# Key products of a pair of heads in two PSUM banks, issued alternately from the two row halves of the array

## The chip, the cores and the metric

The program runs on one core of one Trainium2 chip. The metric is the device time of one execution in microseconds (us). Three executions of the kernel before took 2318.74, 2316.63 and 2325.38 us (median 2318.74).

## What is computed

Two blocks, one after the other, on 512 latent and 256 context positions of width 1024. The first block has an RWKV-7 layer and a differential attention layer; the second has two hybrid attention layers. The change lies in the RWKV-7 layer, in which every one of 16 heads of 64 carries a 64x64 state along the positions, once forward and once backward:

```python
def step(S, inp):
    r_t, w_t, k_t, v_t, kk_t, a_t = inp
    sa = jnp.einsum("bhvk,bhk->bhv", S, kk_t)
    S = (S * w_t[:, :, None, :]
         - sa[..., None] * (kk_t * a_t)[:, :, None, :]
         + v_t[..., None] * k_t[:, :, None, :])
    return S, jnp.einsum("bhvk,bhk->bhv", S, r_t)
```

The streams r, k, v and the decays come from one projection of the normalised input (`h @ w_in`, 34 blocks of 128 columns) with a token shift and two low-rank products; the read-out normalises, gates and projects the result.

## The kernel before

The recurrence is done in chunks of 64 positions. `scan` weaves several generators into one program; each `yield` hands over to the next by a table of virtual times. A scheduler then fixes the order of the instructions on each engine, so what stands in the queues is neither the text's order nor decided on the chip. The parts that matter here:

- **Projection** (`Scan.dense`, `Scan.project`, matmul at L246). Each of the 34 projections has two groups of 24 matmuls of 384 columns, one PSUM bank per group (`pj`, tag "pj", `PJ` = 4 banks). ScalarE takes a bank out (L296 and L297; L351 and L352 for the gate, the last projection of each of eight feature blocks). `px` (tag "x", `6 - PJ` = 2 banks) serves the transposes of the values (L341, copied at L343) and the norms. After the eight blocks come the memory keys and values (`memory`, transposes at L400).
- **Preparation** (`Scan.prep` and `Scan.products`), 48 times: four pairs of feature blocks, three groups of four chunks, two blocks, two directions. The low-rank products go to a bank `ps_g` (L526). Then `products` multiplies the pair's keys: for head h = 0, which lies in partitions 0 to 63, four matmuls (L579), one per chunk, with 64 rows of contraction, 128 stationary and 128 moving columns, into the one bank `ps_b`; VectorE masks that bank out in three instructions (L585 to L587); then the same for h = 1 from partitions 64 to 127. Four transposes (L584) go to `ps_g` and ScalarE copies them (L590). A float32 matmul stands as two records in the trace, so a preparation has 16 records of L579.
- **Inversion** (`Scan.invert`), six times, one for eight preparations: an elimination of 31 steps on VectorE and GpSimd (from the transpose L641 over L655 and L657 to the transpose L661) and then four rounds of small matmuls (L669, L669, L682, L682) through the bank `ps_v` (`psv`) with copies between.
- **Chain** (`Scan.chain`), 48 steps, each one chunk for eight states (c0 at L733, c1 at L768, further products at L744, L757, L778, L791). Steps 4k to 4k+3 need inversion k // 2. Preparation n from the 25th on is put after step 4 (n // 4 - 3) in the program, so the two take turns.
- **Read-outs** and pieces of the modulation (`ada`, L85) run beside the chain; after it comes the dense part (L1079 and on), which has no line of the change.

PSUM has eight banks. During the projection: `ps_g` and `ps_b` in the pool `ppa`, four `pj` and two `x`. During the chain: `ppa` keeps its two, and `ppb` has six: the chain's three, `ps_m`, a second `ps_g` and `ps_v`. `psg` takes `ppa` and `ppb` in turn, and as each preparation asks twice, its low-rank products always get the one and its transposes always the other.

Of the kernel before, what the change touches and what calls it, by code (L numbers as in the profile page):

```python
# [8 lines left out]
FT = mybir.dt.float32  # L9
# [6 lines left out]
PSUM = bass.MemoryType.PSUM  # L16
# [189 lines left out]
class Scan:  # L206
# [14 lines left out]
        return self.pp.tile([128, 512], FT, name="ps_pj", tag="pj", bufs=PJ)  # L221

    def px(self):
        return self.pp.tile([128, 512], FT, name="ps_x", tag="x", bufs=6 - PJ)

    def s3(self, name):
        return self.dp.tile([128, 768], FT, name=name, tag="s3", bufs=SB)
# [254 lines left out]
        return pool.tile([128, 512], FT, name="ps_g", tag="g", bufs=1)  # L482

    def psv(self):
        if CH == 2 and self.ppb:
            return self.psm()
        return (self.ppb or self.ppa).tile([128, 512], FT, name="ps_v", tag="v" if self.ppb else "g", bufs=1)

    def psm(self):
        return self.ppb.tile([128, 512], FT, name="ps_m", tag="m", bufs=1)  # L490
# [72 lines left out]
    def products(self, p, g, jd, n, up, bk, al):  # L563
        E, nc = self.E, self.E.nc
        V, A, P = nc.vector, nc.scalar, nc.tensor
        b, u0 = n // 8, n % 8 * 4
# [5 lines left out]
        mask = self.maskg[:, 0:64].unsqueeze(1).to_broadcast([128, 4, 64])  # L572
        mask_r = self.maskg[:, 64:128].unsqueeze(1).to_broadcast([128, 4, 64])
        rbk = up.tile([128, 2, 4, 64], FT, name="rbk", bufs=8)
        for h, q in ((0, 0), (1, 64)):
            pb = self.ppa.tile([128, 4, 128], FT, name="ps_b", tag="b", bufs=1)
            e, o = q + 64, 64 - q
            for c in range(4):
                P.matmul(pb[:, c, :], bk[q:e, c].rearrange("p s t -> p (s t)"), al[q:e, c, h:3:2 - h, :], start=True,  # L579
                         stop=True, tile_position=(q, 0))  # L580
            if h:
                ps = self.psg()
                for c in range(4):
                    P.transpose(ps[:, c * 128:c * 128 + 128], bk[:, c].rearrange("p s t -> p (s t)"), E.ident)  # L584
            V.tensor_tensor(lb[q:e, u0:u0 + 4, :], pb[q:e, :, 0:64], mask[q:e], OP.mult)  # L585
            V.tensor_tensor(al[o:o + 64, :, h, :], pb[o:o + 64, :, 0:64], mask[o:o + 64], OP.mult)
            V.tensor_tensor(rbk[:, h], pb[:, :, 64:128], mask_r, OP.mult)  # L587
            yield 0
# [341 lines left out]
TB, TV = 3, 3  # L930
XB, OB = 2, 5
AN, AB, AT, AP = 0, 1, 7, -300
PJ = 4
BG = 1
VSB = 1
ZO = 0
# [3 lines left out]
CH = 1  # L940
# [3 lines left out]
def scan(E, stack):  # L944

    tc = E.tc
    right = dict(side="right", bufs=1, reuse_waits="tile")
    left = dict(bufs=1, reuse_waits="tile")
    S = Scan(E)
    ada = [(0, m) for m in range(16, 24)] + [(1, m) for m in range(24)]  # L950
    with ExitStack() as k, ExitStack() as t, ExitStack() as a:
# [24 lines left out]
        def early():  # L976
# [2 lines left out]
            pool = stack.enter_context(tc.tile_pool(name="dn", **left))  # L979
            D.append(Dense(E, pool, stack.enter_context(tc.tile_pool(name="dn_ps", space=PSUM, **left))))  # L980
            S.pt = t.enter_context(tc.tile_pool(name="tp", **left))
            D[0].W.split(0)
            yield lambda: S.read >= 3
            D[0].load_y(E.Y, 0, 6, 2)
# [945 lines left out]
```

## Time and profile before

| | us |
|---|---|
| median of three executions | 2318.74 |
| the profiled execution's own time | 2326.66 |
| its span, first to last instruction | 2324.6 |
| TensorE busy (PE) | 2106.3 (91%) |
| VectorE busy (DVE) | 1567.2 (67%) |
| ScalarE busy (ACT) | 1167.2 (50%) |
| GpSimd busy (POOL) | 686.0 (30%) |
| matmuls of L579, 768 records | 127.4 |
| mean granted TensorE clock | 0.93 |

Busy time counts a stretch once if several records overlap in it. The trace's durations of matmuls include the way through the array, so two matmuls in a row overlap in it and the distance between their starts is what a matmul costs the engine. The granted clock is 1.00 at 2.4 GHz and 0.50 at 1.2 GHz.

### The profile page before, as it was taken

To read this page: it belongs to the slowest core of one execution; us is meant where nothing else is said; L and a number is where in the kernel's file an instruction comes from. 1 tells how busy PE (TensorE), PEld (TensorE's weight loads), DVE (VectorE), ACT (ScalarE), POOL (GpSimd) and SP (SyncE) were. 2 spreads that over 40 slices of the span, in tenths; PEclk is the share of its full clock that TensorE was granted. 3 is DMA by queue.
4 is the path that set the end of the run, shared out by engine and by line. 5 is a ranking of instruction groups with operands and counts; after the bars stand their busy time and mean duration, and the time that the engine had idled before them with its cause. 6 is when DMAs were issued, how large, how long until landed. Compare 5 with 4: busy or idle time off the path is not lost.

```text
span 2324.6 us, 49071 instructions
## 1 busy us (share of the span) xinstructions
PE 2106.3 (91%) x18920; PEld 1867.2 (80%) x18920; DVE 1567.2 (67%) x3937; ACT 1167.2 (50%) x2634; POOL 686.0 (30%) x993
## 2 busy tenths in 40 slices
PE   7999999986899988886989999997899998999989
PEld 3989899975776776664888898987788987888878
DVE  5478868986288877723487767864676674677673
ACT  4455456563255544331255565664455564466652
POOL 0133523433036262321222223323223232032321
PEclk9999999986998788887999999998999999999999
DMA  7467456347544333153321111121312222321132
GB/s 245 136 204 227 144 188 216 105 151 230 184 135 130 90 110 101 54 181 93 134 93 55 47 58 44 42 85 48 114 64 82 67 78 91 119 80 66 60 100 82
DMA packets 190713, 263.60 MB, mean 113 GB/s; under 512 B 16145, under 2 KB 137489, under 8 KB 190353
## 3 DMA queue, kind: packets, MB, share of 16 engines
q1 hardware_dynamic: 190480, 260.48, 34.9%
q8 instruction: 149, 2.44, 0.4%
q14 instruction: 84, 0.68, 0.1%
HBM read 197.24 MB, written 63.18 MB: 112 GB/s over the span
## 4 chain that ended last, share of the span: by engine, by line
PE 47%; DVE 13%; DMA 4%; ACT 3%; issue 3%; POOL 1%; SPq 1%; ACTq 0%; DVEq 0%; POOLq 0%
PE ps_pj L1079 26%; PE ps_s L1376 3%; PE ps_m L85 2%; PE ps_t L1759 2%; PE ps_b L579 1%; PE ps_t L1586 1%; PE ps_s L1079 1%; PE ps_t L1745 1%; DMA w_raw<-in_wd_dram 1%; PE ps_t L1346 1%; DMA w_raw<-att 1%; PE ps_t L1575 1%; DVE ut L657 1%; PE ps_o L744 1%; PE ps_c L733 1%
## 5 line engine op out<-in xcount | busy, mean ns | idle before, releaser
L1079 PE MATMUL ps_pj<-w_hi,act 128*128 128x256 f32 x3264 | 645.5, 292 | 17.9 <-ACT act L1459 4.6
L1079 PEld LDWEIGHTS ps_pj<-w_hi,act 128*128 128x128 f32 x3264 | 529.5, 195 | 31.0 <-ACT act L1459 6.7
L1079 PE MATMUL ps_pj<-w_lo,act 128*128 128x256 f32 x1632 | 470.8, 289 | 0.0
L1079 PEld LDWEIGHTS ps_pj<-w_lo,act 128*128 128x128 f32 x1632 | 319.1, 196 | 0.6 <-issue 0.2
L246 PE MATMUL ps_pj<-h,b_hi 128*128 128x384 f32 (+1 forms) x1216 | 316.6, 341 | 2.7 <-ACT gh L352 1.5
L246 PEld LDWEIGHTS ps_pj<-h,b_hi 128*128 128x128 f32 x1216 | 220.0, 193 | 8.6 <-ACT gh L352 2.7
L246 PE MATMUL ps_pj<-h,b_lo 128*128 128x384 f32 (+1 forms) x608 | 206.9, 341 | 0.3 <-DVE b_lo L190 0.3
L1058 ACT CAST w_hi<-w_raw 128x1024 fp32r<-128x1024 f32 x120 | 121.0, 1050 | 58.9 <-DMA w_raw<-in_wd_dram 28.4
L1060 DVE TENSOR_TENSOR w_lo<-w_raw,w_hi 128x1024 fp32r<-128x1024 f32 x90 | 122.7, 1371 | 41.0 <-ACT w_hi L1058 40.3
L1079 PE MATMUL ps_pj<-act,w_hi 128*128 128x256 f32 x768 | 146.2, 286 | 0.0
L1735 POOL TENSOR_SCALAR p<-p,r 128x128 f32<-128x128 f32 (+2 forms) x64 | 71.8, 1122 | 239.3 <-DVE r L1729 156.7
L1060 POOL TENSOR_TENSOR w_lo<-w_raw,w_hi 128x1024 fp32r<-128x1024 f32 x30 | 72.8, 2428 | 234.3 <-ACT w_hi L1058 234.3
L579 PE MATMUL ps_b<-al,bk 64*128 64x128 f32 x768 | 127.4, 309 | 12.2 <-DVE rbk L587 10.7
L579 PEld LDWEIGHTS ps_b<-al,bk 64*128 64x128 f32 x768 | 105.7, 208 | 33.9 <-issue 21.0
L1079 PEld LDWEIGHTS ps_pj<-act,w_hi 128*128 128x128 f32 x768 | 120.9, 191 | 0.4 <-issue 0.2
L246 PEld LDWEIGHTS ps_pj<-h,b_lo 128*128 128x128 f32 x608 | 117.1, 193 | 3.6 <-issue 1.3
L547 POOL TENSOR_TENSOR s<-bk,src 64x256 f32<-64x256 f32 x96 | 76.9, 801 | 126.8 <-DVE bk L544 114.3
L1079 PE MATMUL ps_pj<-act,w_lo 128*128 128x256 f32 x384 | 109.6, 286 | 0.0
L1302 POOL TENSOR_TENSOR hx<-hx,ctab 128x256 f32<-128x256 f32 x80 | 68.0, 870 | 139.7 <-DVE ht L1300 82.5
L1565 POOL TENSOR_TENSOR p<-p 128x768 f32<-128x768 f32 x32 | 61.1, 1908 | 155.2 <-ACT p L1564 95.2
L1376 PE MATMUL ps_s<-k_s,q_hi 128*128 128x256 f32 (+2 forms) x256 | 91.2, 365 | 15.3 <-ACT p L1555 5.7
L85 PE MATMUL ps_m<-ada_s,cs 128*2 128x128 f32 x512 | 76.7, 314 | 13.4 <-DMA ada_s<-in_ada_w_dram 11.8
(323 smaller groups left out, 4920.0 us busy)
## 6 DMA issues: line engine op xcount, KB each, us to landing
w_raw<-in_wd_dram SPq DMA_DIRECT2D x120, 512.0 KB, 4.4
b_raw<-in_blocks_dram SPq DMA_DIRECT2D x84, 256.0 KB, 3.0
src<-streams SPq DMA_DIRECT2D x48, 384.0 KB, 3.6
ada_s<-in_ada_w_dram SPq DMA_DIRECT2D x32, 512.0 KB, 4.4
vs<-streams SPq DMA_DIRECT2D x48, 256.0 KB, 3.4
ada_w<-in_ada_w_dram SPq DMA_DIRECT2D x8, 1024.0 KB, 11.2
lr<-lora SPq DMA_DIRECT2D x96, 64.0 KB, 3.0
streams<-k SPq DMA_DIRECT2D x32, 192.0 KB, 2.8
```

The lines of the kernel that those rows point to most:

```text
L85: nc.tensor.matmul(ps[0:2, 0:128 * n], E.cs[:, kb, :], w(kb), start=(kb == 0), stop=(kb == 7))
L246: E.nc.tensor.matmul(ps[gi][:, :m], w[:, kb % 4, :], h[:, kb, :], start=(n[gi] == 1), stop=(n[gi] == 24))
L547: G.tensor_tensor(v3(rev(s))[a:a + 64], ut[a:a + 64, 1 if a == 0 else 0], v3(rev(r))[a:a + 64], OP.mult)
L579: P.matmul(pb[:, c, :], bk[q:e, c].rearrange("p s t -> p (s t)"), al[q:e, c, h:3:2 - h, :], start=True, stop=True, tile_position=(q, 0))
L1058: nc.scalar.copy(hi[:, a:a + 4], raw)
L1060: e.tensor_tensor(lo[:, a:a + 4], raw, hi[:, a:a + 4], OP.subtract)
L1079: E.nc.tensor.matmul(ps, a(kb), b(kb), start=(k == 0), stop=(k == 23))
L1302: G.tensor_tensor(w4(x), w4(x), cb, OP.mult)
L1376: P.matmul(ps, q[i][:, 2 * j + h, c], k[h][:, j, a:a + n], start=(i == 0), stop=(stop and i == 1))
L1565: G.tensor_tensor(ps_[0], ps_[0], ps_[1], OP.add)
L1735: G.tensor_scalar(t, t, r[:, h:h + 1], None, OP.mult)
L1759: P.matmul(ps[h * 64:h * 64 + 64, :128], v[:, kb, o:o + 64], pt[:, h, kb, :], start=(kb == 0), stop=(kb == nk - 1), tile_position=(0, h * 64))
```

## The change

The h = 0 and h = 1 products go to two banks (tags "b0" and "b1"), are written in one loop over the chunks, and so alternate between rows 0 to 63 and rows 64 to 127 of the array; VectorE's masking follows behind all eight. The bank for it is taken from two places. `PJ` falls from 4 to 3 and `px` keeps two banks. During the chain, `ps_v` has no bank of its own and shares `ppb`'s `ps_g` (tag "g"); at the end, when `ppa` is closed, a pool of its own (`tp_ps`) gives `psv` a bank.

```diff
     def px(self):
-        return self.pp.tile([128, 512], FT, name="ps_x", tag="x", bufs=6 - PJ)
+        return self.pp.tile([128, 512], FT, name="ps_x", tag="x", bufs=5 - PJ)
...
     def psv(self):
-        if CH == 2 and self.ppb:
-            return self.psm()
-        return (self.ppb or self.ppa).tile([128, 512], FT, name="ps_v", tag="v" if self.ppb else "g", bufs=1)
+        if self.pt:
+            return self.ppt.tile([128, 512], FT, name="ps_v", tag="v", bufs=1)
+        return (self.ppb or self.ppa).tile([128, 512], FT, name="ps_v", tag="g", bufs=1)
...
         rbk = up.tile([128, 2, 4, 64], FT, name="rbk", bufs=8)
+        pbs = [self.ppa.tile([128, 4, 128], FT, name="ps_b", tag="b%d" % h, bufs=1) for h in range(2)]
+        for c in range(4):
+            for h, q in ((0, 0), (1, 64)):
+                P.matmul(pbs[h][:, c, :], bk[q:q + 64, c].rearrange("p s t -> p (s t)"), al[q:q + 64, c, h:3:2 - h, :],
+                         start=True, stop=True, tile_position=(q, 0))
         for h, q in ((0, 0), (1, 64)):
-            pb = self.ppa.tile([128, 4, 128], FT, name="ps_b", tag="b", bufs=1)
-            e, o = q + 64, 64 - q
-            for c in range(4):
-                P.matmul(pb[:, c, :], bk[q:e, c].rearrange("p s t -> p (s t)"), al[q:e, c, h:3:2 - h, :], start=True,
-                         stop=True, tile_position=(q, 0))
+            pb, e, o = pbs[h], q + 64, 64 - q
...
-PJ = 4
+PJ = 3
...
             S.pt = t.enter_context(tc.tile_pool(name="tp", **left))
+            S.ppt = t.enter_context(tc.tile_pool(name="tp_ps", space=PSUM, **left))
```

Lines behind L578 move on by one (L579 becomes L578, L584 L585, L669 L670, L682 L683, L733 L734, L768 L769). The scheduler's order changes in the whole program.

TensorE's queue during the projection, at the end of the second gate and the start of the next projection, whose two groups are `ps_pj_1477` and `ps_pj_1478`. Before, the second group began while the first was still running, and here stand rows of the first group's end with the first head's burst of one preparation:

```order
L246 MATMUL ps_pj_1477<-h_97,b_lo_1436 128x384
L246 MATMUL ps_pj_1477<-h_97,b_hi_1435 128x384
L579 MATMUL ps_b_1771<-al_1723,bk_1647 128x128 x3
L341 MATMUL ps_x_1367<-ident_75,vr_1363 128x128 x4
L579 MATMUL ps_b_1771<-al_1723,bk_1647 128x128
L584 MATMUL ps_g_1797<-ident_75,bk_1647 128x128 x4
L246 MATMUL ps_pj_1477<-h_96,b_hi_1435 128x384
```

Now, the last four products of the same preparation (the four ahead of them read the same), and the same transposes L341:

```order
L578 MATMUL ps_b_1771<-al_1723,bk_1647 128x128
L578 MATMUL ps_b_1772<-al_1723,bk_1647 128x128
L578 MATMUL ps_b_1771<-al_1723,bk_1647 128x128
L578 MATMUL ps_b_1772<-al_1723,bk_1647 128x128
L585 MATMUL ps_g_1797<-ident_75,bk_1647 128x128 x4
L341 MATMUL ps_x_1367<-ident_75,vr_1363 128x128 x4
L526 MATMUL ps_g_1850<-lr_1851,lw_1445 128x256
L526 MATMUL ps_g_1850<-lr_1854,lw_1445 128x256
L246 MATMUL ps_pj_1478<-h_97,b_hi_1403 128x384
```

The first group is complete before the burst, the eight products of both heads stand together and alternate between the two banks, and the second group starts only behind the transposes L341.

TensorE's queue in the chain at the fourth inversion (`ps_v`), step 24 of the chain. Before:

```order
L584 MATMUL ps_g<-ident,bk 128x128 x4
L669 MATMUL ps_v<-ut,lb 32x32 x32
L579 MATMUL ps_b<-al,bk 128x128 x4
L866 MATMUL ps_m<-bdc,sq 128x2 x4
L526 MATMUL ps_g<-lr,lw 128x256 x2
L682 MATMUL ps_v<-lb,ut 32x32 x32
L860 MATMUL ps_m<-osum,bd_102 128x512
L579 MATMUL ps_b<-al,bk 128x128 x4
L584 MATMUL ps_g<-ident,bk 128x128 x4
```

Now:

```order
L683 MATMUL ps_v<-lb,ut 32x32 x32
L85 MATMUL ps_m<-ada_s,cs 2x128 x8
L769 MATMUL ps_c<-rhs,lb 64x64
L683 MATMUL ps_v<-lb,ut 32x32 x32
L90 MATMUL ps_m<-ident,ada_r 128x2
L769 MATMUL ps_c<-rhs,lb 64x64 x7
L779 MATMUL ps_z<-xz,bkt 64x64
L792 MATMUL ps_o<-rbk,xz 64x64
L85 MATMUL ps_m<-ada_s,cs 2x128 x8
L779 MATMUL ps_z<-xz,bkt 64x64 x7
L792 MATMUL ps_o<-rbk,xz 64x64 x7
L585 MATMUL ps_g<-ident,bk 128x128 x4
```

Before, preparations stand between the inversion's rounds, and 37 were through their products ahead of the first round; now none stands between them, 34 are through, and the transposes of the 33rd (`ps_g`) come behind the last round. At the fifth inversion 45 were through before and 42 are now; at the sixth all 48 in both, but the sixth comes at step 38 of the chain before and at step 40 now, the 48th preparation at step 34 and now at step 38. When the last matmul of L246 is issued, 20.5 preparations stood ahead of it before and 24 now.

## Rows read from the trace of the kernel before

**Rows 1.** Busy time by stretch: start:end and length, engines, granted clock, DMA share, GB/s.
```profile
121.00:506.00 385.00, 377.52 (x2728) 347.85 (x2727) 312.12 (x655) 216.59 (x450) 148.16 (x271) 0.97 0.56 180
506.00:545.00 39.00, 23.34 (x98) 17.72 (x98) 29.15 (x70) 17.57 (x33) 12.46 (x27) 0.57 0.62 199
...
642.00:770.00 128.00, 117.81 (x1520) 92.89 (x1517) 107.05 (x249) 65.02 (x152) 63.36 (x130) 0.91 0.44 132
770.00:816.00 46.00, 43.78 (x469) 33.52 (x464) 36.94 (x87) 24.04 (x45) 7.46 (x12) 0.67 0.24 69
...
924.00:986.00 62.00, 52.45 (x978) 42.12 (x973) 43.26 (x116) 25.52 (x43) 20.73 (x66) 0.89 0.20 57
...
1108.00:2324.60 1216.60, 1119.72 (x8762) 1043.68 (x8761) 813.08 (x2216) 655.49 (x1565) 324.83 (x269) 0.96 0.23 77
```

**Rows 2.** The same view, PE and PEld alone, of L246, then of L579.
```profile
121.00:506.00 385.00, 278.88 (x1488) 252.81 (x1488) 0.97 0.56 180
121.00:506.00 385.00, 48.31 (x328) 40.21 (x328) 0.97 0.56 180
```

**Rows 3.** Timeline of PE, a burst of L579 alone: start, length, engine, line.
```profile
145.65 0.60 PE L246 MATMUL ps_pj<-h,b_hi 128*128 128x384 f32 x2
146.18 1.16 PE L579 MATMUL ps_b<-al,bk 64*128 64x128 f32 x8
147.26 0.45 PE L246 MATMUL ps_pj<-h,b_lo 128*128 128x384 f32 x1
```

**Rows 4.** Timeline of PE, L526 and L579 from opposite row halves.
```profile
707.73 0.48 PE L526 MATMUL ps_g<-lr,lw 64*128 64x256 f32 x1
707.74 0.48 PE L579 MATMUL ps_b<-al,bk 64*128 64x128 f32 x2
...
708.51 0.38 PE L579 MATMUL ps_b<-al,bk 64*128 64x128 f32 x2
```

**Rows 5.** Timeline of ACT at the second gate's first bank.
```profile
167.28 0.59 ACT L343 COPY vt<-ps_x 128x512 f32<-128x512 f32 x1 [1.70 <-PE ps_x L341]
...
168.14 0.50 ACT L352 ACTIVATE gh<-ps_pj 128x384 f32<-128x384 f32 x1
```

**Rows 6.** By stretch, L246 alone: a gate's last matmul to its first bank's release.
```profile
160.40:168.70 8.30, 6.09 (x36) 5.80 (x35) 1.00 0.52 158
...
415.20:425.70 10.50, 9.06 (x48) 7.83 (x46) 1.00 0.34 102
```

**Rows 7.** Timelines: the chain's first fetch on SP, its first product on PE.
```profile
526.64 0.50 SPq L611 DMA_DIRECT2D al<-ahead  x1
...
544.83 1.29 PE L733 MATMUL ps_c<-xz,al 128*64 128x64 f32 x16 [8.98 <-POOL itmp L655]
```

**Rows 8.** Timeline of PE, L246 at the lower and at the higher clock.
```profile
142.34 0.84 PE L246 MATMUL ps_pj<-h,b_hi 128*128 128x384 f32 x2
142.98 0.38 PE L246 MATMUL ps_pj<-h,b_lo 128*128 128x384 f32 x1
143.20 0.51 PE L246 MATMUL ps_pj<-h,b_hi 128*128 128x384 f32 x2
143.55 0.34 PE L246 MATMUL ps_pj<-h,b_lo 128*128 128x384 f32 x1
```

**Rows 9.** Timeline of DVE, start and end of the fourth and sixth eliminations.
```profile
714.11 1.25 DVE L641 STREAM_TRANSPOSE ut<-ut 128x1024 f32<-128x1024 f32 x1 [0.86 <-ACT ut L639]
...
780.51 2.06 DVE L661 STREAM_TRANSPOSE ut<-ut 128x1024 f32<-128x1024 f32 x1
...
936.48 1.25 DVE L641 STREAM_TRANSPOSE ut<-ut 128x1024 f32<-128x1024 f32 x1 [3.17 <-ACT ut L639]
...
962.07 2.02 DVE L661 STREAM_TRANSPOSE ut<-ut 128x1024 f32<-128x1024 f32 x1
```

**Rows 10.** Timeline of PE, the fourth inversion's first round and the product that needed it.
```profile
784.37 1.20 PE L669 MATMUL ps_v<-ut,lb 32*32 32x32 f32 x64
...
803.38 0.47 PE L768 MATMUL ps_c<-rhs,lb 64*64 64x64 f32 x2
```

## Prediction

> **What bounds the kernel now.** The busy table by stretch comes first, because the mean shares hide three different limits. From 121 to 506 us TensorE is busy for 377.5 of 385 us at a granted clock of 0.97 [rows 1]: the projection is bound by TensorE, and L579 takes 48.3 us of it in 328 records, which is 20.5 preparations [rows 2]. From 506 to 545 us TensorE has 23 busy us in 39 at 0.57 [rows 1]: the last preparations, the memory's transposes and the chain's first fetches pass one after the other. From 642 us (step 12 of the chain) to 770 us (step 24), TensorE is busy for 118 of 128 us and VectorE for 107 [rows 1], so neither has much room. From 770 to 816 us (step 24 to step 25) the chain waits for its fourth inversion. The dense part behind 1108 us, 1217 us long, has no line of the change; I take it as the same, with 5 us either way for its new order. The timelines then give the prices. I sum against the profiled execution's 2326.66 us, which lies 7.9 us above the median of 2318.74.
>
> **Row halves in parallel.** A burst of eight records of L579 on one row half takes 1.08 us from its start to the next matmul's [rows 3], about 0.13 us a record. The two L246 ahead of it take 0.53 us where two plain ones take 0.35 [rows 3, 8], so a burst among L246 costs some 1.3 us with the change of tile on both sides. Does the other row half come free? L526 and L579 of opposite halves already stand side by side: they start 10 ns apart, and four records of L526 and eight of L579 are all started within 0.78 us [rows 4]. At 0.13 us a record the eight alone would need 1.04. So 16 alternating records should take what eight do, and a preparation loses one burst, 1.3 us. For 20.5 preparations that is 27 us; a few bursts overlap already with L526, and I take -24.
>
> **More preparations ahead.** The new order puts 3.5 more of them into the projection. Each costs low-rank products (a burst's worth, 1.3), one double burst (1.3) and transposes (half a burst), an estimate of 3.2 us: +11.
>
> **The third bank of the projection.** Three `pj` banks are enough unless an eviction is late, and the gate's is: at the second gate it stands in ScalarE's queue behind the copy at 167.28 us, which waits for the transposes L341, and its first bank is free at 168.64 [rows 5]. Between a gate's last matmul and that moment the projection has started 36 to 48 matmuls in the four gates that I counted, of which the least and the most are shown [rows 6]; with one spare bank it can do 24. The 12 to 24 left over, at 0.175 us [rows 8], make 2.1 to 4.2 us a gate as the worst case, and nothing is the best, since the new order has the transposes nearer to the gate and other work ahead of the second group. I take 1.5 for each of eight gates: +12, with bounds of 0 and 34.
>
> **From the projection to the chain.** The chain's first product follows its first fetch by 18.2 us [rows 7]. The fetch comes 20.6 us after 506, since the last 3.5 preparations stand among the memory's transposes. With these preparations done earlier, I estimate 8 us for the memory's rest and 18 for the fetch: 26 instead of 39, -13. Sum until the chain starts: -24 + 11 + 12 - 13 = -14.
>
> **In the chain.** Steps 12 to 24 lose one burst in ten preparations, by the burst's 1.3 us, with a little of it behind VectorE: -12. Then the bank that `ps_v` gives up. Transposes that follow an inversion in the program wait for its last round, so preparations and inversion no longer run side by side. Side by side, the fourth elimination took 66 us from 714 to 780; with no preparation beside it, the sixth took 26 [rows 9]. From its first round to the product that needs it the fourth inversion took 19 us [rows 10]. So step 24 should find its elimination finished and last 26 us (19 and the product's ordinary way) instead of 46: -20. At the fifth inversion the two effects cancel: shorter elimination, later preparations. At the sixth, preparations 43 to 48 run in five chain steps, by 128 us for twelve steps [rows 1] less their gain some 50 us, and the elimination of 26 and rounds of 19 follow: 95 us from step 33 to the product of step 40. Before, that was the 62 us from 924 to 986 [rows 1] and 2 more: +31, as the sixth inversion was hidden and no longer is. Sum in the chain: -12 - 20 + 31 = -1.
>
> **Sum.** -14 - 1 = -15: 2326.66 becomes 2311.7 for the profiled execution, and 2318.7 becomes **2304 us** as a median, 0.6% faster. Differences of about 0.5% (12 us) are what a measurement of this kernel can tell from no change.
>
> **A rule weighed.** Eight stretches of L246 with little waits between them could also cost clock: L246 starts every 0.32 us at 1.2 GHz against 0.175 at 2.4 [rows 8], and the stretch in which TensorE was busy for 60% had 0.57 granted [rows 1]. The rows of the projection say otherwise so far: 0.97 with four banks in turn [rows 1]. The Trainium skill, "TensorE: Matmul & The Clock Gate", section "A second HAM failure mode: psum-queue depth-cycling", says that a kernel that cycles through its PSUM banks can idle briefly between groups often enough for the clock to go up and down. By that rule every gate's wait would also be followed by matmuls at the lower clock, which is a price in the second rival; by the row it is nothing, and I go by the row.
>
> **Rivals.** (1) Slower: the shared `ps_v` bank makes preparations and inversions one serial path, and the work that VectorE does not do beside the elimination it lacks later. Then step 24 is not shortened (0 instead of -20) and steps 12 to 24 gain nothing (0 instead of -12) while the sixth inversion costs its 31: 2304 + 32 = 2336. For it: the new queue holds back three preparations at each inversion, and VectorE is busy for 107 of 128 us. Against it: the step-24 wait is the longest in the chain, and what lengthens it is just the work that moves away. It decides from 12 us on at step 40 if step 24 stays as it is. (2) No change: the third bank eats the projection's gain. With the worst 34 us for the gates, the sum rises by 22 to 2326; with half of that, or ten L246 at the lower clock behind each gate (1.4 us each, 11 in all), it is 2315. For it: late gate evictions in every block; against it: the scheduler has filled the place. (3) Much faster: the sixth inversion is done by step 40 after all, because preparations run faster than I think: 2304 - 31 = 2273. For it: TensorE, busy for 118 of 128 us, is what the change relieves. (4) The halves do not overlap for these products: only the saved change of tile remains, 0.2 us for each of 20.5 preparations, and 20 us of the first term and the 12 in the chain go: 2336. Rows 4 speak against it.
>
> **Chances.** My forecast has 0.40, of which I give 0.08 to the side within 0.5%; rival 1 0.25, rival 2 0.17, rival 3 0.15, rival 4 0.03. Faster by over 0.5%: 0.32 + 0.15 = 0.47. Within: 0.08 + 0.17 = 0.25. Slower: 0.25 + 0.03 = 0.28. The range from 2270 to 2340 takes in all four rivals' times; worse gates together with rival 1 stay out above, and a gain in every term below.
>
> **What would show it.** Right: the records of the key products start in pairs some 10 ns apart and a double burst takes about 1.1 us; the last L246 near 505 us, the first product of the chain near 531; step 24 to step 25 in about 26 us; a wait of some 25 us at step 40. Wrong: idle time of several us in front of L246 behind each gate; a clock clearly below 0.97 in the projection; step 24 still as long as 46 us, or no wait at step 40.

## The result, and the profile after

The changed kernel is slower: 2349.97 us against 2318.96 us (medians of four runs each). The ratio is estimated at 1.0117 (95% interval 1.0073 to 1.0162, which holds the 1.0134 of these two medians). A second comparison, of six runs with 23, gave 1.0091 (1.0069 to 1.0112). The forecast of 2304 us lay on the other side, and the time lies outside its range. The profiled execution took 2354.66 us, 28.0 more than that of before, and its span is 28.2 us longer.

A ledger of starts on TensorE in the two profiled executions tells where. Each difference is compared with the sum of the prediction's terms up to that place. The term for the sixth inversion runs from step 33 to the product of step 40, so the sum has no value of its own at step 40.

| | before | after | difference | predicted |
|---|---|---|---|---|
| last L246 | 505.7 | 529.8 | +24.1 | -1 |
| chain's first product (L733, now L734) | 544.8 | 554.8 | +10.0 | -14 |
| step 24 | 769.9 | 770.2 | +0.3 | -26 |
| step 25 | 815.8 | 791.9 | -23.9 | -46 |
| step 32 | 889.0 | 884.4 | -4.6 | -46 |
| step 33 | 923.6 | 916.3 | -7.3 | -46 |
| step 40 | 986.4 | 993.1 | +6.7 | |
| step 41 | 999.0 | 1034.0 | +35.0 | -15 |
| chain's last product | 1056.3 | 1096.5 | +40.2 | -15 |
| first L1173 (now L1175) | 1103.3 | 1125.2 | +21.9 | -15 |
| end of the span | 2324.6 | 2352.8 | +28.2 | -15 |

Three places lose more than the sum had: the projection (24 us), the stretch from step 25 to step 33 (17 us), and the stretch from step 33 to step 41 (42 us where 31 were expected). After the chain 18 us come back.

Stretches of the kernel after, by the busy table (columns as in [rows 1]):

```profile
121.00:506.00 385.00, 358.54 (x2667) 329.98 (x2666) 309.35 (x647) 210.82 (x442) 151.52 (x274) 0.95 0.56 178
...
649.90:770.20 120.30, 101.91 (x1454) 80.41 (x1449) 100.48 (x231) 55.17 (x124) 53.77 (x117) 0.87 0.37 107
770.20:791.90 21.70, 17.43 (x318) 12.67 (x316) 4.57 (x10) 5.61 (x12) 0.72 (x1) 0.78 0.32 95
791.90:916.30 124.40, 96.66 (x1361) 73.71 (x1360) 96.79 (x217) 58.16 (x125) 53.59 (x115) 0.82 0.35 105
916.30:993.10 76.80, 68.41 (x878) 53.07 (x877) 55.21 (x137) 33.96 (x75) 26.62 (x60) 0.90 0.33 95
993.10:1034.00 40.90, 23.63 (x413) 17.04 (x412) 23.35 (x53) 13.77 (x21) 12.00 (x34) 0.71 0.37 116
1125.20:2352.80 1227.60, 1121.01 (x8768) 1045.95 (x8768) 816.81 (x2221) 657.14 (x1567) 321.94 (x269) 0.96 0.24 77
```

From 121 to 506 us TensorE is idle for 26.5 us, where it was idle for 7.5 [rows 1]. The same view of L246 alone, then of the key products (L578) alone:

```profile
121.00:506.00 385.00, 272.10 (x1428) 248.45 (x1427) 0.95 0.56 178
...
121.00:506.00 385.00, 28.54 (x336) 23.34 (x336) 0.95 0.56 178
```

Against [rows 2] the key products take 20 us less for even half a preparation more, so the row halves do what was said of them. Yet 60 records of L246 fewer are done by 506 us. Against the 20 us stand 19 us of new idle time and some 4.5 us of longer busy time: a record of L246 takes 190.5 ns of it instead of 187.4. The granted clock is 0.95 instead of 0.97, but the clock's share of the 4.5 us was not told apart from that of more frequent breaks: the second comparison's profile of the same kernel has 190.6 ns at 0.96.

The timeline of PE shows an isolated double burst, between L246 and the transposes L585:

```profile
362.96 0.51 PE L246 MATMUL ps_pj<-h,b_hi 128*128 128x384 f32 x2
363.40 1.16 PE L578 MATMUL ps_b<-al,bk 64*128 64x128 f32 x16
364.49 0.66 PE L585 MATMUL ps_g<-ident,bk 128*128 128x128 f32 x4
```

Sixteen records pass in 1.09 us, what eight took [rows 3]. What TensorE waits for in that stretch is in the groups of PE by line, 121 to 506 us (busy, mean ns, then idle time ahead and what ended most of it); the last row is the first group in the kernel before, 121 to 505 us:

```profile
L246 PE MATMUL ps_pj<-h,b_hi 128*128 128x384 f32 (+1 forms) x952 | 254.0, 347 | 5.9 <-ACT gh L352 5.9
L246 PE MATMUL ps_pj<-h,b_lo 128*128 128x384 f32 (+1 forms) x476 | 163.4, 344 | 5.0 <-POOL b_lo L190 2.8 <-DVE b_lo L190 2.1
L578 PE MATMUL ps_b<-al,bk 64*128 64x128 f32 x336 | 28.5, 301 | 3.3 <-DVE bk L553 3.3
...
L341 PE MATMUL ps_x<-ident,vr 128*128 128x128 f32 x84 | 13.7, 290 | 2.8 <-DVE k L322 1.8 <-POOL vr L338 1.0
L268 PE MATMUL ps_x<-ones,sq 128*128 128x2 f32 x92 | 11.2, 246 | 2.3 <-ACT sq L264 2.3
...
L246 PE MATMUL ps_pj<-h,b_hi 128*128 128x384 f32 (+1 forms) x988 | 257.8, 341 | 2.5 <-ACT gh L352 1.5 <-ACT b_hi L189 0.8
```

Only 5.9 us are a gate's eviction (L352), 1.5 before. The rest are waits for VectorE, GpSimd and ScalarE at many places.

In the chain, the timeline of DVE around the fourth, fifth and sixth eliminations: L642 is the first transpose of one, L662 the last, and the L588 shown is the last masking of a group's eighth preparation.

```profile
763.11 2.04 DVE L662 STREAM_TRANSPOSE ut<-ut 128x1024 f32<-128x1024 f32 x1
...
846.11 0.41 DVE L588 TENSOR_TENSOR rbk<-ps_b,maskg 128x256 f32<-128x256 f32 x1
...
851.89 1.25 DVE L642 STREAM_TRANSPOSE ut<-ut 128x1024 f32<-128x1024 f32 x1 [1.18 <-ACT ut L640]
891.62 2.01 DVE L662 STREAM_TRANSPOSE ut<-ut 128x1024 f32<-128x1024 f32 x1 [0.70 <-POOL ut L658]
...
973.98 0.39 DVE L588 TENSOR_TENSOR rbk<-ps_b,maskg 128x256 f32<-128x256 f32 x1
...
977.56 1.25 DVE L642 STREAM_TRANSPOSE ut<-ut 128x1024 f32<-128x1024 f32 x1 [2.21 <-ACT ut L640]
1006.42 2.02 DVE L662 STREAM_TRANSPOSE ut<-ut 128x1024 f32<-128x1024 f32 x1
```

And the timeline of PE at the fourth, fifth and sixth inversions, with the products c1 (L769) that need the fourth and the sixth and the start of step 41 (L734); the two rows at the end are the fifth and sixth inversions of the kernel before:

```profile
767.66 1.92 PE L670 MATMUL ps_v<-ut,lb 32*32 32x32 f32 x64
...
782.37 0.47 PE L769 MATMUL ps_c<-rhs,lb 64*64 64x64 f32 x2
...
893.69 1.20 PE L670 MATMUL ps_v<-ut,lb 32*32 32x32 f32 x64 [2.72 <-DVE ut L662]
...
1008.50 1.92 PE L670 MATMUL ps_v<-ut,lb 32*32 32x32 f32 x64 [6.70 <-DVE ut L662]
...
1024.38 0.47 PE L769 MATMUL ps_c<-rhs,lb 64*64 64x64 f32 x2
1034.02 0.48 PE L734 MATMUL ps_c<-xz,al 128*64 128x64 f32 x2 [3.84 <-DVE xz L787]
...
892.59 1.20 PE L669 MATMUL ps_v<-ut,lb 32*32 32x32 f32 x64
...
964.14 1.92 PE L669 MATMUL ps_v<-ut,lb 32*32 32x32 f32 x64 [5.03 <-DVE ut L661]
```

They show one path in turns: eight preparations, elimination, rounds, then the next eight. Before, the eighth masking of the fifth and sixth groups ended at 821.9 and 933.3 us; now at 846.5 and 974.4. The fourth inversion's rounds start 16.7 us earlier than in [rows 10], the fifth's at 893.7 (892.6 before), the sixth's 44 us later than the 964.1 of before.

Where the preparations went is in the records of their key products, from step 24 to 25 and from 25 to 32 (PE and PEld alone, 16 records a preparation), before and after:

```profile
769.90:815.80 45.90, 11.29 (x56) 9.60 (x56) 0.67 0.24 69
815.80:889.00 73.20, 13.74 (x80) 11.32 (x80) 0.88 0.40 121
...
770.20:791.90 21.70, 0.00 (x0) 0.00 (x0) 0.78 0.32 95
791.90:884.40 92.50, 12.06 (x128) 10.06 (x128) 0.85 0.36 106
```

The wait of step 24 took in 3.5 preparations before and takes in none now. Between the starts of steps 25 and 32 stand eight instead of five, and that stretch takes 19 us more.

### The profile page after: what moved, and what is told of

It reads as the page before. It is cut to its first block, busy times and chain, and to the rows that moved or that the text cites. A ratio compares the mean times of both kernels' runs of the same rounds, so it can differ in the third digit from the quotient of the medians.

```text
span 2352.8 us, 49027 instructions
## 1 busy us (share of the span) xinstructions
PE 2066.5 (88%) x18920; PEld 1834.1 (78%) x18920; DVE 1569.9 (67%) x3937; ACT 1164.2 (49%) x2634; POOL 681.5 (29%) x993
## 5 line engine op out<-in xcount | busy, mean ns | idle before, releaser
L246 PE MATMUL ps_pj<-h,b_hi 128*128 128x384 f32 (+1 forms) x1216 | 320.3, 344 | 8.5 <-ACT gh L352 5.9
L246 PEld LDWEIGHTS ps_pj<-h,b_hi 128*128 128x128 f32 x1216 | 222.3, 195 | 16.6 <-ACT gh L352 7.0
L246 PE MATMUL ps_pj<-h,b_lo 128*128 128x384 f32 (+1 forms) x608 | 207.5, 343 | 5.8 <-POOL b_lo L190 3.7
L246 PEld LDWEIGHTS ps_pj<-h,b_lo 128*128 128x128 f32 x608 | 118.6, 195 | 9.2 <-POOL b_lo L190 4.4
L189 ACT CAST b_hi<-b_raw 128x512 fp32r<-128x512 f32 x84 | 52.0, 620 | 97.9 <-PE ps_pj L246 87.7
L85 PE MATMUL ps_m<-ada_s,cs 128*2 128x128 f32 x512 | 79.3, 318 | 16.4 <-DMA ada_s<-in_ada_w_dram 13.1
L578 PE MATMUL ps_b<-al,bk 64*128 64x128 f32 x768 | 72.2, 307 | 15.0 <-DVE bk L553 10.5
```

The lines of the kernel that those rows point to most:

```text
L85: nc.tensor.matmul(ps[0:2, 0:128 * n], E.cs[:, kb, :], w(kb), start=(kb == 0), stop=(kb == 7))
L189: nc.scalar.copy(hi, raw)
L246: E.nc.tensor.matmul(ps[gi][:, :m], w[:, kb % 4, :], h[:, kb, :], start=(n[gi] == 1), stop=(n[gi] == 24))
L578: P.matmul(pbs[h][:, c, :], bk[q:q + 64, c].rearrange("p s t -> p (s t)"), al[q:q + 64, c, h:3:2 - h, :], start=True, stop=True, tile_posi ...
```

## The experiments

**One payment at a time.** Two kernels start from the one before. The first takes only the projection's bank, the second only shares `ps_v`'s:

```diff
-PJ = 4
+PJ = 3
...
-        return self.pp.tile([128, 512], FT, name="ps_x", tag="x", bufs=6 - PJ)
+        return self.pp.tile([128, 512], FT, name="ps_x", tag="x", bufs=5 - PJ)
```

> The kernel before with PJ = 3 and two px banks; the key products as before, the eighth bank unused. Theory A (the two payments for the bank cost more than the row halves bring): L246 loses what it lost in the changed kernel, some 22 us (296.1 us from start to start against 273.5, most of it idle time), so the last L246 starts near 528 us, the chain near 565, and the whole is 20 to 25 us longer, near 2341. Theory B (three banks are enough; the alternating burst and its new waits made the projection longer): the last L246 within 5 us of 505.7, the whole within 5 us of 2319.

Measured: 1.0079 (1.0058 to 1.0101), 18 us; last L246 at 527.6, chain at 559.7. Theory A: the last L246 to the microsecond, the chain 5 us earlier and the whole 2 us less than it had. The groups of PE by line, 121 to 506 us, then the busy table of that stretch:

```profile
L246 PE MATMUL ps_pj<-h,b_hi 128*128 128x384 f32 (+1 forms) x946 | 252.5, 347 | 3.0 <-ACT gh L352 3.0
...
L579 PE MATMUL ps_b<-al,bk 64*128 64x128 f32 x311 | 47.6, 292 | 7.5 <-DVE bk L553 4.5 <-DVE rbk L587 3.0
...
L341 PE MATMUL ps_x<-ident,vr 128*128 128x128 f32 x84 | 14.0, 290 | 5.3 <-POOL vr L338 5.3
...
121.00:506.00 385.00, 367.63 (x2616) 337.89 (x2615) 296.61 (x623) 203.92 (x425) 145.08 (x265) 0.96 0.54 174
```

Without any row halves waits of the same kind appear, 17.4 us of idle time in all: the bank costs mostly away from the gates, where TensorE's next instruction in order needs something of VectorE or GpSimd.

```diff
-        return (self.ppb or self.ppa).tile([128, 512], FT, name="ps_v", tag="v" if self.ppb else "g", bufs=1)
+        if self.pt:
+            return self.ppt.tile([128, 512], FT, name="ps_v", tag="v", bufs=1)
+        return (self.ppb or self.ppa).tile([128, 512], FT, name="ps_v", tag="g", bufs=1)
```

> The kernel before with ps_v in the second ps_g bank during the chain; PJ = 4 and the key products as before, one bank unused. Theory A (sharing makes preparations and inversions one serial path): the projection within 5 us of before; step 24 lasts some 25 us instead of 46; from step 25 to step 40 it takes some 30 us more than the 171 of before, and step 40 waits about 28 us longer; together 30 to 40 us slower, 2350 to 2358. Theory B (the later preparations in the changed kernel come from the new burst's waits for VectorE, not from the shared bank): steps 25 to 41 within 10 us of before, the whole 2300 to 2320.

Measured: 1.0165 (1.0137 to 1.0193), 38 us; the last L246 at 508.7 and the chain at 545.6, nearly as before. The busy table from step 24 to 25, 25 to 32, 32 to 33, 33 to 40 and 40 to 41:

```profile
761.90:784.20 22.30, 17.60 (x371) 13.70 (x367) 10.35 (x19) 11.12 (x17) 0.14 (x1) 0.85 0.17 50
784.20:862.90 78.70, 72.46 (x933) 57.75 (x932) 65.85 (x144) 43.68 (x100) 37.23 (x62) 0.94 0.46 135
862.90:927.70 64.80, 39.77 (x475) 26.15 (x474) 31.49 (x72) 13.04 (x23) 20.02 (x54) 0.65 0.23 69
927.70:993.70 66.00, 59.27 (x793) 47.91 (x792) 46.53 (x113) 33.02 (x72) 16.24 (x32) 0.92 0.23 65
993.70:1051.00 57.30, 32.08 (x430) 22.47 (x429) 33.74 (x74) 13.39 (x20) 24.91 (x66) 0.59 0.40 121
```

Step 24 shrinks, steps 32 and 40 now wait for 65 and 57 us, with TensorE busy for 40 and 32 of them; the eighth maskings of the fifth and sixth groups come at 846.2 and 985.6. Theory A again, at the upper end. The two payments together, 56 us, are two to three times what the change costs (31 and 21 us by the medians of the two comparisons), so the rest of it gains, if the two payments simply add.

**Which bank, and the alternation alone.** From the changed kernel: `PJ = 4` again, which leaves one px bank (the first hunk); and the products head after head with both banks kept (the second):

```diff
-PJ = 3
+PJ = 4
...
-        for c in range(4):
-            for h, q in ((0, 0), (1, 64)):
+        for h, q in ((0, 0), (1, 64)):
+            for c in range(4):
```

> The changed kernel with PJ = 4 and therefore one px bank instead of two. Theory A (the third pj bank was what the projection paid with): L246 starts follow as before, the last one 15 to 25 us earlier than 529.8, the whole 15 to 25 us faster than the changed kernel, 2325 to 2335. Theory C (what the projection lacks is any bank: the transposes of the values and the norms need two px banks as much): the last L246 at 525 us or later, the whole 2345 to 2365.

> The changed kernel with both banks, but the four products of h = 0 first and then the four of h = 1: only the alternation of row halves is taken away. Theory A (the halves overlap and bring about 1.1 us a preparation): L578 busy for about 125 us instead of 72.2, the last L246 15 to 25 us later, the whole 15 to 35 us slower than the changed kernel, 2365 to 2385. Theory B (the alternating burst is itself what costs): within 5 us of the changed kernel's 2350 or faster.

One px bank: 1.0182 (1.0144 to 1.022), last L246 at 533.6: theory C, the second px bank is no more spare than the fourth pj bank. Head after head: 1.0125 (1.0099 to 1.0152), not to be told from the changed kernel. The profile still shows the alternation at work: last L246 at 542.3 (12.5 us later) and the chain at 572.9. Of the 18 us that alternation is worth at the chain's start, 5 are left at the end of step 40's wait, which comes at 1038.7 there and at 1034.0 in the changed kernel. So theory A held for the projection in kind (12.5 us where it had 15 to 25) and not for the total. Nor was L578 as slow as expected (92.9 us busy, not 125). The timeline of PE has a double burst head after head:

```profile
344.04 1.61 PE L578 MATMUL ps_b<-al,bk 64*128 64x128 f32 x16
345.57 0.45 PE L246 MATMUL ps_pj<-h,b_lo 128*128 128x384 f32 x1
```

It takes 1.53 us to the next start (median of 34 whole bursts 1.64), between the 1.09 of alternation and the 2.16 of two bursts apart. So half the gain comes without alternating: in all 34 the first record of h = 1 starts ahead of the last three of h = 0, and one change of tile is saved. That VectorE now masks behind all eight products, and not behind each head's four, was not tried by itself.

**Borrowed banks.** The bank for h = 1 is taken in turn from banks that have other users, with `PJ = 4` and `ps_v` on its own:

```diff
-        pbs = [self.ppa.tile([128, 4, 128], FT, name="ps_b", tag="b%d" % h, bufs=1) for h in range(2)]
+        pbs = [self.ppa.tile([128, 4, 128], FT, name="ps_b", tag="b", bufs=1),
+               (self.psg() if self.ppb else self.px()).rearrange("p (c t) -> p c t", c=4)]
```

In the other three it is px in the projection only, ps_g in the chain only, and ps_g in both.

> Both payments undone and the row halves kept: PJ = 4, two px banks and ps_v with its own bank as in the kernel before; the bank for h = 1 is borrowed, from px during the projection and from the two ps_g banks in turn during the chain. Theory A (the halves gain some 25 to 30 us, and the two payments, +18 and +38 us when made alone, eat it): the last L246 near 495 to 505 us, step 24 as long as before (some 46 us), step 40 without its wait, 10 to 30 us faster than the kernel before. Theory C (any bank taken costs as much as the third pj bank, borrowed or not): the last L246 at 520 us or later, and no faster than the kernel before.

> The kernel before with the row halves in the projection alone: h = 1 goes to a px bank while the projection runs, PJ = 4; in the chain the products stay head after head in one bank, and ps_v has its own. Theory A: the same last L246 as in the run that borrows in both places, 495 to 505 us, the chain from some 530 us on as before (step 24 near 46 us, step 40 near 12), 10 to 20 us faster than the kernel before. Theory C: the last L246 at 520 us or later, 10 to 30 us slower than the kernel before.

> The kernel before, with the row halves in the chain alone: there h = 1 goes to the ps_g bank whose turn it is, so that no bank is taken from pj or ps_v; during the projection the products stay head after head in the one ps_b. Theory A (without the payments the halves gain): the projection as before (last L246 near 506 us), a preparation one burst shorter, the chain from its first step to its last 10 to 16 us below the 511.5 of before, the whole 8 to 16 us faster. Theory D (VectorE, not TensorE, sets the pace of the preparations in the chain): the chain within 5 us of before and no gain; if the third turn in ps_g binds, slower by up to 20 us.

> As the run that borrows ps_g in the chain, and in the projection too: there is only one ps_g then, which takes the low-rank products, h = 1's products and the transposes in turn, and the inversion's rounds. No bank is taken from pj or px. Theory A: 1.0 us a preparation from the row halves, some of it given back to waits for ps_g: last L246 490 to 505 us and the whole 10 to 30 us faster than before. Theory C (in the projection every bank counts, borrowed ones too, because VectorE masks late and holds it): the last L246 at 520 us or later and no faster than before.

Measured: 1.0442 (1.0412 to 1.0472), 1.0466 (1.0439 to 1.0494), 1.0035 (1.0016 to 1.0053), 1.0205 (1.0177 to 1.0233). A borrowed px bank is far worse than either theory had it: the last L246 at 619 us. The order puts preparations ahead of the projection (24 are through their products by 506 us, with 1300 records of L246; before, 20.5 with 1824), which is then not there to fill the waits. The busy table of the run in the projection only, then of the kernel before:

```profile
281.00:320.00 39.00, 14.63 (x276) 11.48 (x278) 22.11 (x47) 11.80 (x21) 8.43 (x21) 0.54 0.22 80
...
281.00:320.00 39.00, 38.94 (x452) 37.08 (x452) 21.84 (x38) 19.39 (x32) 4.74 (x8) 0.96 0.43 137
```

TensorE works 15 of 39 us through an inversion's rounds, at 0.54 granted, and starts no L246; before, it was busy there for 38.9 at 0.96. With ps_g borrowed in the chain alone the halves bring nothing (chain 509.9 us, 511.5 before): theory D's time. Whether VectorE sets the pace there or the third turn in ps_g takes the gain was not measured. With ps_g in both, the last L246 comes at 495.8, in theory A's range, and the chain at 522.7; but only 18 preparations have begun ahead of that L246 (22 before), the rest push the chain's end to 1088.8, and the total is theory C's.

**Another partner for `ps_v`.** From the changed kernel: `ps_v` in its own bank, ps_g reduced to one in the chain; and `ps_v` in the bank of `ps_m`.

```diff
-        pool = self.ppb if self.ppb and (self.ng % 2 or self.pt) else self.ppa
+        pool = self.ppt if self.pt else self.ppa
...
-        return (self.ppb or self.ppa).tile([128, 512], FT, name="ps_v", tag="g", bufs=1)
+        return self.psm() if self.ppb else self.ppa.tile([128, 512], FT, name="ps_v", tag="g", bufs=1)
```

> The changed kernel with ps_v in its own bank again; in the chain ps_g keeps one bank instead of two, so that a preparation's low-rank products and the transposes take turns in it. Theory A (steps 25 to 41 lost their time to the bank that preparations and inversions share): the projection as in the changed kernel (last L246 near 530), step 24 to step 25 back to some 45 us, step 40 below 15 us, steps 25 to 40 within 10 us of the 171 of before; 10 to 25 us faster than the changed kernel, within 0.5% of the kernel before. Theory D (it is the preparations' own late start that costs, whatever bank ps_v has): step 40 still waits over 20 us, and the time is that of the changed kernel or longer.

> The changed kernel with ps_v in the bank of ps_m instead of the second ps_g, so that inversions share a bank with read-outs and modulation and not with preparations. Theory A (sharing with the preparations' transposes is what makes the path serial): preparations run beside the inversion again; the sixth elimination ends before step 40 does, its wait falls from 41 us to under 20; 10 to 25 us faster than the changed kernel. Theory D (any shared bank delays the rounds as much): the wait of step 40 stays over 30 us or step 24 or 32 grows by as much; the changed kernel's time or longer.

The own bank: 1.0127 (1.0094 to 1.0161). Step 40 falls to 13 us and the chain ends at 1074.0, 22 us earlier than in the changed kernel, as theory A said; but the first L1175 starts at 1124.7, where it did, and nothing is won. Step 24 takes 14 us and steps 25 to 40 take 195, where theory A had 45 and 171. Step 32 takes 58 us (the fifth elimination now runs beside preparations and takes 73 us), and the modulation's products, which the long wait at step 40 had taken in, follow the chain again, the last of them 19 us behind it. With `ps_m`: 1.038 (1.034 to 1.0419), theory D. The fifth elimination is over early, but its rounds stand behind modulation in the shared bank (timelines of DVE, then PE):

```profile
850.00 2.11 DVE L662 STREAM_TRANSPOSE ut<-ut 128x1024 f32<-128x1024 f32 x1
```

```profile
957.97 1.20 PE L670 MATMUL ps_m<-ut,lb 32*32 32x32 f32 x64 [0.25 <-DVE mod L96]
```

**The bank or the order.** First, the kernel before with a rule of order and no shared bank:

```diff
         yield lambda: n < 4 * NSK + 8 or (self.pb is not None and self.done >= n // 4 - 3)
+        yield lambda: n < 34 or self.inverted >= (n - 2) // 8
```

> The kernel before with all its banks (four pj, ps_v its own, one ps_b) and one more rule for the order: from the 35th preparation on, a preparation may follow in the program only when the inversion of the group before has been written, as the shared bank brings it about. Theory A (the path preparations, elimination, rounds in turn is what costs, and no bank as such): the same picture as with the shared bank alone: eighth preparation of the fifth and sixth groups masked some 25 and 50 us later than before (821.9 and 933.3), step 24 near 22 us, step 40 over 40 us, 25 to 40 us slower than the kernel before. Theory E (the shared bank costs by its own waits, not by the order): within 10 us of the kernel before.

> The changed kernel itself once more, beside the same runs of the kernel before, for a narrower interval: 1.0 to 1.5% slower. If it were below 0.5%, the first comparison would have been the chip's.

The rule: 1.003 (1.0011 to 1.0049), no serial path. But 38 and 45 transposes stand ahead of the fourth and fifth inversions' first rounds, against 38 and 46 before: with nothing to bind them, the scheduler moved the preparations forward again, so the run did not test what it was for. The reverse does. In the next three the shared bank stays and inversions are written later in the chain, with 3, 3 and 1.5 units of virtual time for each of their steps instead of 0.2; the second has no other part of the change:

```diff
+        streams[0][3] = 3
         S.pb = k.enter_context(tc.tile_pool(name="sb", **right))
```

> The changed kernel, all its banks as they are, but in the chain an inversion is written more slowly (3 units of virtual time for each of its steps instead of 0.2), so that 39 and 46 preparations' transposes stand in front of the first rounds of the fourth and fifth inversions, as in the kernel before (38 and 46), instead of 32 and 40. Theory A (the shared bank costs through the order that it fixes: who is written first is served first): the eighth preparations of the fifth and sixth groups masked some 5 to 15 us after 822 and 933, step 24 again over 40 us, step 40 under 20 us, the whole 8 to 20 us faster than the changed kernel, 2328 to 2340; what is left is the projection's. Theory E (the bank itself: any wait of rounds and transposes for one another costs the same): step 24 and step 40 together as long as in the changed kernel or longer, and no gain.

> The kernel before with the shared ps_v bank alone (38 us slower when it was tried), and an inversion written as slowly as in the run above: 39 and 46 transposes in front of the fourth and fifth inversions. Theory A: the 38 us go: within 12 us of the kernel before, step 40 under 20 us. Theory E: still 25 to 40 us slower.

> The changed kernel with 1.5 units for each step of an inversion: 35 and 44 transposes in front of the fourth and fifth. Theory A: between the two: step 24 some 25 to 35 us, step 40 15 to 30 us, and the time at or below the one with 3 units, 2320 to 2340, since part of the shorter step 24 is kept without the late sixth inversion. Theory E: the changed kernel's time, 2345 or more.

The shared bank alone, inversions late: 1.004 (1.0016 to 1.0064) instead of 1.0165. The busy table of the same five stretches:

```profile
763.90:818.50 54.60, 47.18 (x497) 35.36 (x491) 47.11 (x111) 31.01 (x54) 16.23 (x33) 0.72 0.27 78
818.50:895.90 77.40, 68.38 (x884) 52.93 (x884) 60.68 (x133) 32.94 (x78) 38.80 (x86) 0.87 0.45 134
895.90:928.20 32.30, 30.59 (x485) 23.69 (x484) 17.71 (x41) 12.11 (x25) 4.84 (x7) 0.84 0.28 81
928.20:994.60 66.40, 55.51 (x1006) 42.55 (x1005) 38.05 (x97) 21.28 (x40) 18.80 (x64) 0.92 0.23 67
994.60:1002.90 8.30, 6.68 (x106) 5.45 (x106) 3.33 (x8) 2.70 (x5) 0.00 (x0) 0.91 0.76 220
```

Step 24 is long again, steps 32 and 40 are not, and the eighth maskings come at 803.0 and 929.5. With the same banks some 29 of the 38 us go when the order is changed: theory A. In the changed kernel the middle value gives 1.0033 (1.0014 to 1.0053), two thirds of the loss, with steps 24, 32 and 40 of 19, 29 and 12 us (24 and 40 a little shorter than expected). With 3 units the changed kernel stays at 1.0128 (1.0088 to 1.0167), against theory A's range: there the fifth elimination ends at 840.6 but its rounds start at 913.7, and steps 41 to 44 take 56 us (30 before) among read-outs. In this kernel too late is as dear as too early.

**The change in the chain alone.** Projection as before; in the chain `ps_v` shares ps_g and its bank takes h = 1, with inversions written as before, with 1.5 and with 1 unit:

```diff
+        pair = bool(self.ppb)
+        pbs = [self.ppa.tile([128, 4, 128], FT, name="ps_b", tag="b", bufs=1)]
+        if pair:
+            pbs.append(self.ppb.tile([128, 4, 128], FT, name="ps_b", tag="b1", bufs=1))
```

> The change in the chain alone: during the projection four pj banks, two px banks and the products head after head in one ps_b, as before; in the chain ps_v shares the second ps_g bank, and the bank so freed takes h = 1's products, which alternate with those of h = 0. Beside the shared bank alone (38 us slower than before) it tells what the row halves are worth in the chain, beside the changed kernel (20 to 27 us slower than before) what the change in the projection costs. Theory A (projection +10 at the chain's start, of which the waits for the fourth and fifth inversions hide a part; halves worth some 15 us in a chain that is bound by preparations): 15 to 25 us slower than before. Theory F (the row halves are worth nothing in the chain, as in the run that borrowed ps_g): 33 to 43 us slower.

> The same with 1.5 units for each step of an inversion in the chain, which brought the changed kernel from 1.0% above the kernel before to 0.3%. Theory A: without the projection's payment too, the chain starts at 545 instead of 555 and the whole is at or below the kernel before, from 10 us faster to 3 us slower. Theory F: 10 to 20 us slower than before.

> The same with 1 unit: 34 and 42 transposes ahead of the fourth and fifth inversions instead of 35 and 44. Theory A: step 24 near 25 us, step 40 some 20 us, the whole from 5 us faster to 10 us slower than before. Theory F: 15 to 30 us slower.

Measured: 1.0054 (1.003 to 1.0077), 1.0121 (1.0088 to 1.0155), 1.0073 (1.0048 to 1.0098). The first, a little better than theory A had it, lies 1.1% under the shared bank alone, so in that serial chain the halves are worth some 25 us (the sixth group's eighth masking at 959.1, 985.6 without them; the scheduler's order differs too), and about 0.5% under the changed kernel, which is the projection's part (0.4 to 0.6% by the two comparisons of that kernel; the chain's start differs by 10.5 us). The other two were expected near the kernel before or ahead of it, and are behind it: by 26 us, more than either theory had, and by 17, theory F's time. Their chains end at 1072.8 and 1068.2, and the part from the first L1173 on (moved by nine lines there) takes 1235.5 and 1237.8 us instead of 1221.3, with no line changed there. That accounts for the profiled executions only: the one with 1.5 units is the fastest of its six (2339.6 us, median 2351.2). Whether the rest is the order or the execution stays open, and no version here beats the kernel before.

## Why the prediction was wrong

**Row halves in parallel: right in kind, and nearly in size.** A preparation's products take 1.09 us instead of two bursts of 1.08, a gain of 1.07 where 1.3 was taken: 22 us for 20.5 preparations against -24. Some 3 us go back, since L526 lost its partner (0.23 us a record from start to start before, 0.27 now).

**Third bank of the projection: the mis-sized term.** I priced gates, 1.5 us each, +12. The bank alone moved the last L246 by 22 us (with 21.5 preparations ahead of it instead of 20.5) and the chain's start by 15. In the changed kernel more is missing: -22 and +3 for the halves and my estimate of +11 for the preparations ahead make -8, and +24 was measured, so 32 us are left for this term. The 10 us between 22 and 32 belong to the bank together with the rest of the change, or to the estimate of +11; no run separates them. The bounds of 0 and 34 held this, but the mechanism I counted is the smaller one: late gates are 3.0 us of TensorE's idle time with the bank alone and 5.9 in the changed kernel, 1.5 before. The reading that fits is that a projection with less room ahead stops covering the late results of VectorE and GpSimd: more than three quarters of the new idle time (19 us by 506 us) stands in front of other instructions than a gate's. VectorE was busy for 312 of the 385 us [rows 1], which I left out of this term. The clock had a small part at most: 0.95 for 0.97 granted, within the 4.5 us of longer busy time. The Trainium skill, "TensorE: Matmul & The Clock Gate", section "A second HAM failure mode: psum-queue depth-cycling", says that a tensor engine that idles briefly and often between groups of matmuls can have its clock go up and down. The trace agrees in direction: 0.95 granted with 26.5 us of idle time, 0.97 with 7.5.

**From the projection to the chain: right.** 25.0 us against 26; the fetch comes 8.3 us behind the last L246 and the first product 16.7 behind the fetch, against 8 and 18.

**Steps 12 to 24: near in number, by luck.** -7.6 us against -12. But the stretch now holds nine preparations instead of 11.5 (144 records of key products for 184), and the shared bank alone, without any row halves, has -6.1 there (121.8 us). Shorter bursts are not what shows; TensorE's idle time rises from 10 to 18 us.

**Step 24: right.** -24.2 us against -20. Its elimination ends at 765.1, ahead of the step at 770.2, and from its first round to the product it takes 14.7 us. The elimination itself took 42 us, not the 26 I had for one undisturbed; two preparations stood beside it.

**"At the fifth inversion the two effects cancel": the step that failed in the chain.** They do cancel for the inversion: its rounds start at 893.7 against 892.6. But a chain that waits for an event at the same time as before cannot keep its lead, and I carried -46 through. The 23.9 us gained by step 25 are 4.6 at step 32 and 7.3 at step 33. In the changed kernel most of it goes ahead of the wait, in the stretch from step 25 to 32, where the preparations run that step 24 no longer takes in. With the shared bank alone the same eight preparations let that stretch pass in 78.7 us, and the lead goes in the wait of step 32, 64.8 us instead of 34.6. So most of the lead, or all of it, is gone by step 33 either way.

**The sixth inversion: right in kind, too small.** I had 95 us from step 33 to the product of step 40; it took 108 (916.3 to 1024.4), where it was 65 before: +43 against +31. From step 33 to the end of the eighth masking it took 58 us where I had 50, then 3 us to the elimination, 31 for it where I had 26, and 16 for the rounds where I had 19.

**Not foreseen: what comes back.** Modulation's last product (L85) stood 16 us behind the chain's end and now stands 0.7 ahead of it, so 18 us of the chain's delay do not reach L1175. The 6 us behind it (1227.6 against 1221.3) lie within the 1216 to 1238 that this part takes in the profiles of all the kernels here. But the second profile of the changed kernel has 1227.0, so they may belong to its order; that stays open.

**Rivals.** The first rival had the mechanism: one serial path of preparations and inversions, and work that VectorE does not do beside the elimination (37 us busy in step 24 before, 4.6 now) and lacks later. Its form was wrong: step 24 was shortened in full, and the loss came from step 25 on. The second rival had the place: its worst price for the third bank, 34 us, is near the 32 of the changed kernel, but most of that does not stand at the gates. Both came together, a case that I had left outside the range. The third rival, a sixth inversion that is done in time, and the fourth, halves that do not overlap, are refuted.

## What to carry to other kernels

A PSUM bank whose own evictions are mostly on time can still be the room in which the scheduler covers other engines' lateness: price its loss by trying it alone, not by the one eviction that the trace shows late. When two loops get a common buffer, the order in which they are written becomes binding; ask whose turn comes first at each handover, and move that order before judging the buffer. Ask what work a wait has been filled with before shortening it, because that work will stand somewhere else. And a lead gained ahead of a wait is worth only as much as the event waited for comes earlier.

## What the runs showed of the hardware

Matmuls on opposite row halves need not alternate to overlap: eight records on one half and then eight on the other, adjacent in the queue, take 1.64 us (median of 34), where the two bursts apart take 2.16 and alternating ones 1.09. They do not start in the order of the queue either: in all 34 bursts the first record on the second half starts ahead of the last three on the first (at 344.49 us, where those three start at 344.59, 344.71 and 344.82).
